# A hybrid encoder block on one core: first loads, value projection, attention values and last output chunk rearranged

## The chip, the cores and the metric

The kernel runs on one core of a Trainium2 chip. The metric is the device time of one execution in microseconds (us). Before the change the median of three runs is 1520.54 us (1519.51 to 1520.96).

## What is computed

The reference takes 512 tokens of width 1024. Everything is float32.

```
xn   = rms_norm(x, ln1)
proj = xn @ w_in                      # 1024 -> 2560: u 512, gate v 512, q 512, k 512, value 512
a    = gelu(u) * (w_s . rms_norm(gelu(v)) + b_s)        # block of 128 positions, 8 groups, masked
b    = softmax(q k^T / 8 + bias[rel]) value             # 8 heads of 64, chunk-causal, chunks of 64
x    = x + concat(a, b) @ w_out
x    = x + peer(rms_norm(x, ln2))     # 8 heads, top 16 of 128x128 experts, rows of two 16384x1024 tables
```

The change touches everything up to `w_out`; the expert part (`peer`) is left as it was.

## The kernel before, in words

The tokens are four tiles of 128 (t = 0 to 3); the model width is eight slices of 128 (k = 0 to 7). A product at full precision is written as three float32r matmuls on high and low parts (`mm3`, lines 117 to 121): a weight block of 128 x 1024 is loaded by SP's queue into `raw` (3 buffers), ScalarE makes `hi` (line 103), VectorE makes `lo` = `raw` - `hi` (line 104); `hi` and `lo` have 5 buffers each. A buffer is written again only when the matmuls that read it are done, so line 103 can wait for TensorE.

1. **Start.** SP's queue loads the gain row `g1`, the first tile of x, three weight blocks and the second tile of x, in this order (lines 185 to 192). `norm_transposed` (lines 131 to 151) squares a tile on ScalarE (137), makes 1/rms on VectorE and ScalarE (126 to 128), scales it on VectorE (`xs`, 140), transposes it on TensorE (145) and splits it into `xh` and `xl` (149, 150).
2. **Projections.** q goes token tile by token tile (lines 199 to 204). k and the values go through `token_major` (169): the loop over k is outside, four PSUM tiles are open at once, and the results are copied out at the end. Between k and the values stands the head norm of q and k (207 to 224): square, sum per head, 1/rms, scale (`qn`), eight transposes, copies to `qkT`.
3. **Gate values.** `gate_values` projects the gate input with `token_major` (96 `mm3` matmuls), then gelu and norm.
4. **Attention and gated product, interleaved** (lines 361 to 380). A step is one token tile and two heads; there are 16. TensorE's order is the program's (`manual_schedule`): in iteration i it does the scores of step i, a piece of the gated projection (iterations 0 to 7) or of the spatial product (8 to 11), the transposes of the weights of step i-2, and the values of step i-3. The softmax weights `pe` are not normalised; `values` multiplies them with `v_sb`, 64 columns wide, and after eight heads VectorE divides by the row sums into `o` (300). `mixed` transposes `o` (312) and splits it into `mh`, `ml`. Four gelus of 512 columns (353) stand behind the spatial product in the program.
5. **Output product.** Two chunks of 512 columns with `token_major`, each added to x on VectorE (402); then the second `norm_transposed` into `xbh`, `xbl`, on which routing (the first step of the expert part) waits.

Outside `manual_schedule` a scheduler sets each engine's order when the program is built, by priorities and its own cost estimates. An engine takes its instructions strictly in that order. What is written where in the program therefore moves instructions of all engines, also those of untouched lines.

Of the kernel before, what the change touches and what calls it, by code (L numbers as in the profile page):

```python
# [8 lines left out]
F32 = mybir.dt.float32  # L9
# [5 lines left out]
ALU = mybir.AluOpType  # L15
# [55 lines left out]
def hybrid_block(tc, x, ln1, w_in, gng, wsT, bsb, qkg, bias, w_out, ln2, wq, skT, uT, ud, vd, out):  # L71
    nc = tc.nc
    ctx = ExitStack()
    with ctx:
# [94 lines left out]
        def token_major(lh, ll, w, evac):  # L169

            pss = [pa() if t < 3 else pu() for t in range(TT)]
            for k in range(KT):
                for t in range(TT):
                    tok = slice(t * P, (t + 1) * P)
                    mm3(pss[t], (lh[:, k, tok], ll[:, k, tok]), w(k), k == 0, k == KT - 1)
            for t in range(TT):
                evac(t, pss[t])


        with tc.tile_pool(name="prea", bufs=1) as prea:  # L180
# [4 lines left out]
            nc.sync.dma_start(g1, bcast_rows(ln1, D))  # L185
            x_t = []
            for t in range(TT):
                xt = prea.tile([P, D], F32, name="x_t", tag="xq", bufs=4)
                nc.sync.dma_start(xt, x_r[t])
# [9 lines left out]
            for t in range(TT):  # L199
                ps = pu()  # L200
                tok = slice(t * P, (t + 1) * P)
                for k in range(KT):
                    mm3(ps, (xh[:, k, tok], xl[:, k, tok]), w0(k), k == 0, k == KT - 1)
                nc.scalar.copy(qk[t][:, 0:CW], ps)
            token_major(xh, xl, chunk_of(w_in, 2 * WA // CW + 1, CW),
                        lambda t, ps: nc.scalar.copy(qk[t][:, CW:2 * CW], ps))
            for t in range(TT):
# [8 lines left out]
                                        r[:, :, None].to_broadcast([P, 16, 64]), op=ALU.mult)  # L216
                for half in range(2):
                    ps = pa()
                    for j in range(4):
                        nc.tensor.transpose(ps[:, j * P:(j + 1) * P],  # L220
                                            qn[:, (4 * half + j) * P:(4 * half + j + 1) * P], ident)
                    nc.scalar.activation(qkT[:, 4 * half:4 * half + 4, t * P:(t + 1) * P],
                                         ps.rearrange("p (j t) -> p j t", t=P), AF.Copy,
                                         scale=qkgt[:, half:half + 1])
            token_major(xh, xl, chunk_of(w_in, 4 * WA // CW, CW),
                        lambda t, ps: nc.scalar.copy(v_sb[t], ps))


        with tc.tile_pool(name="preb", bufs=1) as preb:
# [34 lines left out]
            def weights(t, h, ps):  # L264
# [9 lines left out]
                                     accum_out=st[:, 1, h:h + 1])  # L274
                pes[t, h] = pe
# [11 lines left out]
            def values(t, h):  # L287
                if h == 0:
                    pvs[t] = pa()
                pv = pvs[t]  # L290
                pT = pTs.pop((t, h))
                hd = slice(h * 64, (h + 1) * 64)
# [3 lines left out]
                if h == HB - 1:  # L296
                    r = preb.tile([P, HB], F32, name="rs", tag="rs", bufs=2)
                    nc.vector.reciprocal(r, sts[t][:, 1, :])
                    o = preb.tile([P, WA], F32, name="o", tag="o", bufs=2)
                    nc.vector.tensor_tensor(o.rearrange("p (h d) -> p h d", d=64),  # L300
                                            pv.rearrange("p (h d) -> p h d", d=64),
                                            r[:, :, None].to_broadcast([P, HB, 64]), op=ALU.mult)
                    os[t] = o

            os = {}

            def mixed(t):

                o = os.pop(t)
                ps = pa()  # L310
# [3 lines left out]
                pv = ps.rearrange("p (k t) -> p k t", t=P)  # L314
                nc.scalar.copy(mh[to], pv)
                nc.vector.tensor_tensor(ml[to], pv, mh[to].bitcast(F32), op=ALU.subtract)
# [26 lines left out]
            def spatial():  # L343
# [8 lines left out]
                for m in range(4):  # L352
                    nc.scalar.activation(ugT[:, m, :], ugT[:, m, :], AF.Gelu_apprx_tanh)
# [10 lines left out]
            with tc.manual_schedule(engines={mybir.EngineType.PE}):  # L364
                for i in range(len(steps) + LAG + 3):
# [7 lines left out]
                    if 0 <= i - LAG - 1 < len(steps):  # L373
                        t, hs = steps[i - LAG - 1]
                        for h in hs:
                            values(t, h)
# [14 lines left out]
        with tc.tile_pool(name="prec", bufs=1) as preb:  # L391
# [7 lines left out]
            for c in range(D // CW):  # L399
                cs = slice(c * CW, (c + 1) * CW)  # L400
                token_major(mh, ml, chunk_of(w_out, c, CW),
                            lambda t, ps: nc.vector.tensor_tensor(x2[t][:, cs], x2[t][:, cs], ps, op=ALU.add))
# [353 lines left out]
```

## Time and profile before

| | before |
|---|---|
| median of 3 runs | 1520.54 us |
| the profiled execution | 1516.51 us |
| its span (first to last instruction) | 1514.7 us |
| TensorE busy | 1469.0 us, 97% |
| VectorE busy | 1118.7 us, 74% |
| ScalarE busy | 624.3 us, 41% |
| GpSimd busy | 474.8 us, 31% |

A busy share counts the time in which an instruction of the engine was under way. Matmuls overlap, so TensorE's throughput is read from the distance between the starts of successive matmuls, not from the length of one. A bracket at the end of a timeline row gives the idle time of that engine just before the row, and what ended it.

### The profile page before, as it was taken

How to read it: one execution, taken by the hardware profiler on the slowest of the kernel's cores; microseconds unless marked ns; L12 is line 12 of the kernel's file. 1: busy time of each engine (PE TensorE's matmuls, PEld its weight loads, DVE VectorE, ACT ScalarE, POOL GpSimd, SP SyncE). 2: the span in 40 equal slices, each digit the busy share in tenths (PEclk: the TensorE clock that was granted, in tenths of full speed). 3: DMA queues.
4: the chain of work that ended last, by engine and by line, in shares of the span. 5: the costliest groups of instructions: out<-in, count | busy, mean ns of one | idle time of the engine just before them, and what ended most of it. 6: DMA issues, size and time to landing. Idle time of an engine off the chain costs nothing.

```text
span 1514.7 us, 21441 instructions
## 1 busy us (share of the span) xinstructions
PE 1469.0 (97%) x7817; PEld 1315.6 (87%) x7817; DVE 1118.7 (74%) x2095; ACT 624.3 (41%) x1163; POOL 474.8 (31%) x322
## 2 busy tenths in 40 slices
PE   7899998999989999999999999999999999999998
PEld 5787887888879989999999999999999999998887
DVE  5425626999999986788777777777776877766773
ACT  5439715434446655333333333333333333333331
POOL 0000000000016753054444544444553444443420
PEclk9999999999999999999999999999999999999999
DMA  5341144223336879899898889888888888877881
GB/s 180 112 167 45 53 142 143 92 82 115 101 108 181 231 233 295 320 355 357 315 328 292 316 312 334 301 323 326 292 317 320 319 315 320 311 243 248 312 283 68
DMA packets 151721, 360.02 MB, mean 238 GB/s; under 512 B 11008, under 2 KB 71424, under 8 KB 151616
## 3 DMA queue, kind: packets, MB, share of 16 engines
q1 hardware_dynamic: 114528, 223.64, 43.5%
q0 software_dynamic: 37088, 135.02, 24.4%
q8 instruction: 61, 1.00, 0.3%
q14 instruction: 44, 0.36, 0.1%
HBM read 328.73 MB, written 29.88 MB: 237 GB/s over the span
## 4 chain that ended last, share of the span: by engine, by line
PE 62%; DMA 1%; DVE 0%; ACT 0%; issue 0%; POOL 0%; DVEq 0%; SPq 0%; ACTq 0%
PE pa L683 12%; PE pa L684 12%; PE pa L687 11%; PE pu L119 9%; PE pu L121 9%; PE pu L120 9%; PE pa L577 2%; DMA gd<-gst 1%; DMA gc<-gd 0%; ACT gst L582 0%; POOL bm L571 0%; DVE lo L104 0%; DVE bm L570 0%; ACT hi L103 0%; DVE wl L673 0%
## 5 line engine op out<-in xcount | busy, mean ns | idle before, releaser
L103 ACT ACTIVATE hi<-raw 128x1024 fp32r<-128x1024 f32 x300 | 317.1, 1058 | 538.0 <-PE pu L120 245.1
L104 DVE TENSOR_TENSOR lo<-raw,hi 128x1024 fp32r<-128x1024 f32 x300 | 369.6, 1233 | 173.1 <-ACT hi L103 168.3
L119 PE MATMUL pu<-xbh,hi 128*128 128x384 f32 x1024 | 346.6, 339 | 5.3 <-ACT act L432 5.3
L121 PE MATMUL pu<-xbh,lo 128*128 128x384 f32 x1024 | 345.4, 337 | 0.0
L120 PE MATMUL pu<-xbl,hi 128*128 128x384 f32 x1024 | 345.2, 337 | 0.0
L683 PE MATMUL pa<-hi,wh 128*128 128x512 f32 x768 | 299.2, 390 | 1.1 <-ACT wh L672 1.1
L684 PE MATMUL pa<-lo,wh 128*128 128x512 f32 x768 | 299.0, 389 | 0.0
L626 POOL DMA_INDIRECT row<-in_ud,eint x128 | 188.4, 1472 | 267.0 <-DVE row L628 237.1
L637 POOL DMA_INDIRECT row<-in_vd,eint x128 | 191.5, 1496 | 233.2 <-DVE acc L639 204.0
L687 PE MATMUL pa<-hi,wl 128*128 128x512 f32 x768 | 236.6, 389 | 0.5 <-DVE wl L673 0.5
L119 PEld LDWEIGHTS pu<-xbh,hi 128*128 128x128 f32 x1024 | 192.8, 188 | 8.2 <-ACT act L432 6.2
L120 PEld LDWEIGHTS pu<-xbl,hi 128*128 128x128 f32 x1024 | 192.6, 188 | 1.8
L121 PEld LDWEIGHTS pu<-xbh,lo 128*128 128x128 f32 x1024 | 192.6, 188 | 0.0
L571 POOL TENSOR_TENSOR bm<-bm,gt 128x1024 f32<-128x1024 f32 x48 | 91.1, 1897 | 301.1 <-DVE bm L570 301.1
L639 DVE SCALAR_TENSOR_TENSOR acc<-row,hw,acc 128x1024 f32<-128x1024 f32 x128 | 163.8, 1280 | 13.1 <-DMA row<-in_vd,eint 13.0
L687 PEld LDWEIGHTS pa<-hi,wl 128*128 128x128 f32 x768 | 144.1, 188 | 30.9 <-DVE wl L673 0.8
L683 PEld LDWEIGHTS pa<-hi,wh 128*128 128x128 f32 x768 | 144.2, 188 | 29.6 <-ACT wh L672 1.4
L684 PEld LDWEIGHTS pa<-lo,wh 128*128 128x128 f32 x768 | 144.2, 188 | 28.4
L628 DVE SCALAR_TENSOR_TENSOR row<-row,xb 128x1024 f32<-128x1024 f32 x128 | 155.8, 1219 | 11.7 <-DMA row<-in_ud,eint 11.6
L673 DVE TENSOR_TENSOR wl<-act,wh 128x768 fp32r<-128x768 f32 x64 | 61.2, 958 | 114.4 <-ACT wh L672 114.4
L672 ACT ACTIVATE wh<-act 128x768 fp32r<-128x768 f32 x64 | 54.0, 846 | 152.7 <-PE pa L684 150.8
L577 PE MATMUL pa<-bm,am 128*128 128x128 f32 x768 | 94.3, 276 | 5.4 <-POOL bm L571 3.6
(174 smaller groups left out, 1649.8 us busy)
## 6 DMA issues: line engine op xcount, KB each, us to landing
raw<-in_uT SPq DMA_DIRECT2D x128, 512.0 KB, 5.1
raw<-in_vd SPq DMA_DIRECT2D x128, 512.0 KB, 4.9
gd<-gst SPq DMA_DIRECT2D x48, 512.0 KB, 5.3
gc<-gd SPq DMA_DIRECT2D x32, 768.0 KB, 8.4
raw<-in_w_in SPq DMA_DIRECT2D x20, 512.0 KB, 4.2
raw<-in_wq SPq DMA_DIRECT2D x16, 512.0 KB, 4.5
raw<-in_w_out SPq DMA_DIRECT2D x8, 512.0 KB, 3.6
x_t<-in_x SPq DMA_DIRECT2D x4, 512.0 KB, 5.4
```

The costliest lines, as they stand in the source:

```text
L103: nc.scalar.activation(hi, raw, AF.Copy)
L104: nc.vector.tensor_tensor(lo, raw, hi.bitcast(F32), op=ALU.subtract)
L119: nc.tensor.matmul(ps, lh[0], rh[0], start=first, stop=False)
L120: nc.tensor.matmul(ps, lh[0], rh[1], start=False, stop=False)
L121: nc.tensor.matmul(ps, lh[1], rh[0], start=False, stop=last)
L626: nc.gpsimd.indirect_dma_start(out=row, out_offset=None, in_=ud, in_offset=bass.IndirectOffsetOnAxis(ap=eint[:, j:j + 1], axis=0))
L628: nc.vector.scalar_tensor_tensor(row, row, 1.0, xb0, op0=ALU.mult, op1=ALU.mult, accum_out=hw[:, j:j + 1])
L637: nc.gpsimd.indirect_dma_start(out=row, out_offset=None, in_=vd, in_offset=bass.IndirectOffsetOnAxis(ap=eint[:, j:j + 1], axis=0))
L639: nc.vector.scalar_tensor_tensor(acc0, row, hw[:, j:j + 1], acc0, op0=ALU.mult, op1=ALU.add)
L683: nc.tensor.matmul(accs[t][half], wh[:, b, tok], w[b][0][:, ds_], start=first, stop=False)
L684: nc.tensor.matmul(accs[t][half], wh[:, b, tok], w[b][1][:, ds_], start=False, stop=False)
L687: nc.tensor.matmul(accs[t][half], wl[:, b, tok], w[b][0][:, ds_], start=False, stop=last)
```

## The change

Five edits. The first tile of x is loaded as two halves, by SP's and by ScalarE's queue, and `g1` goes to GpSimd's queue. The value projection is done token tile by token tile inside the loop of the head norm, ahead of each tile's transposes. Each head's weights are divided by their sum right after the exponential (a reciprocal on VectorE, a scaling on GpSimd); the values of two heads are then computed transposed, the head's 64 value columns as the stationary operand, into the two halves of the partitions, so that `o` and its transposes go. The four gelus become one of 2048 columns. The second output chunk is done token tile by token tile.

```diff
-            nc.sync.dma_start(g1, bcast_rows(ln1, D))
...
+                if t == 0:
+
+                    nc.sync.dma_start(xt[:, 0:512], x_r[t][:, 0:512])
+                    nc.scalar.dma_start(xt[:, 512:D], x_r[t][:, 512:D])
+                    nc.gpsimd.dma_start(g1, bcast_rows(ln1, D))
+                else:
+                    nc.sync.dma_start(xt, x_r[t])
...
+            wv = chunk_of(w_in, 4 * WA // CW, CW)
             for t in range(TT):
...
+                ps = pu()
+                tok = slice(t * P, (t + 1) * P)
+                for k in range(KT):
+                    mm3(ps, (xh[:, k, tok], xl[:, k, tok]), wv(k), k == 0, k == KT - 1)
+                nc.scalar.copy(v_sb[t], ps)
                 for half in range(2):
...
-            token_major(xh, xl, chunk_of(w_in, 4 * WA // CW, CW),
-                        lambda t, ps: nc.scalar.copy(v_sb[t], ps))
...
+                nc.vector.reciprocal(st[:, 1, h:h + 1], st[:, 1, h:h + 1])
+                nc.gpsimd.tensor_scalar(pe[:, :nk], pe[:, :nk], st[:, 1, h:h + 1], None, op0=ALU.mult)
...
-                    nc.tensor.matmul(pv[:, hd], pT[:, j * P:(j + 1) * P], v_sb[j][:, hd],
-                                     start=j == 0, stop=j == t)
...
+                    for h, pT in zip(hs, pTh):
+                        nc.tensor.matmul(pv[rows_of(h), pair], v_sb[j][:, h * 64:(h + 1) * 64],
+                                         pT[:, j * P:(j + 1) * P], start=j == 0, stop=j == t)
...
-                for k in range(4):
-                    nc.tensor.transpose(ps[:, k * P:(k + 1) * P], o[:, k * P:(k + 1) * P], ident)
...
-                for m in range(4):
-                    nc.scalar.activation(ugT[:, m, :], ugT[:, m, :], AF.Gelu_apprx_tanh)
+                nc.scalar.activation(ugT, ugT, AF.Gelu_apprx_tanh)
...
+            token_major(mh, ml, chunk_of(w_out, 0, CW), residual(0))
+            token_major(mh, ml, chunk_of(w_out, 1, CW), residual(1), True)
```

With its last argument `token_major` runs the loop over t outside, one PSUM tile at a time. How the change moves instructions is shown at three places.

VectorE at the start, before (`rstd` is 1/rms of a tile, `xs` the scaled tile):

```order
L126 TENSOR_SCALAR rstd_142<-ss_139 128x1
L128 RECIPROCAL rstd_142<-rstd_142 128x1
L140 SCALAR_TENSOR_TENSOR xs_146<-x_t_104,rstd_142,g1_102 128x1024
L104 TENSOR_TENSOR lo_108<-raw_106,hi_107 128x1024
L104 TENSOR_TENSOR lo_114<-raw_112,hi_113 128x1024
```

VectorE at the start, in the changed kernel (`rstd_166` and `xs_170` are of the second tile):

```order
L126 TENSOR_SCALAR rstd_143<-ss_140 128x1
L128 RECIPROCAL rstd_143<-rstd_143 128x1
L104 TENSOR_TENSOR lo_109<-raw_107,hi_108 128x1024
L104 TENSOR_TENSOR lo_115<-raw_113,hi_114 128x1024
L104 TENSOR_TENSOR lo_121<-raw_119,hi_120 128x1024
L126 TENSOR_SCALAR rstd_166<-ss_163 128x1
L128 RECIPROCAL rstd_166<-rstd_166 128x1
L140 SCALAR_TENSOR_TENSOR xs_147<-x_t_103,rstd_143,g1_102 128x1024
L104 TENSOR_TENSOR lo_127<-raw_125,hi_126 128x1024
L140 SCALAR_TENSOR_TENSOR xs_170<-x_t_131,rstd_166,g1_102 128x1024
```

The scaling of the first tile has moved from third place to behind three weight splits and the 1/rms of the second tile. On TensorE the second tile's transposes have moved ahead too: from behind 24 matmuls of the first tile to behind one.

ScalarE in the changed kernel at the end of the gated projection, iterations 7 to 9 (`pe` a head's exponential, `pT` its transposed copy, `hi_1810` a block of `w_out`):

```order
L285 ACTIVATE pe_1201,st_1049<-sc_1197,st_1049 128x256
L103 ACTIVATE hi_1810<-raw_1809 128x1024
L285 ACTIVATE pe_1209,st_1049<-sc_1205,st_1049 128x256
L298 COPY pT_1229<-pu_1226 128x256
L298 COPY pT_1234<-pu_1231 128x256
L354 ACT_TABLE_LOAD
L354 ACTIVATE ugT_95<-ugT_95 128x2048
L285 ACT_TABLE_LOAD
L285 ACTIVATE pe_1252,st_1243<-sc_1248,st_1243 128x384
L285 ACTIVATE pe_1260,st_1243<-sc_1256,st_1243 128x384
L298 COPY pT_1277<-pu_1274 128x256
```

Before, the same place had a gelu of 512 columns and no `hi` in front of it; the other three gelus stood earlier, each between two table loads.

VectorE at the end of the second output chunk, in the changed kernel (last two tiles of the second norm):

```order
L401 TENSOR_TENSOR x2_1677<-x2_1677,pu_1885 128x512
L126 TENSOR_SCALAR rstd_1990<-ss_1987 128x1
L104 TENSOR_TENSOR lo_2064<-raw_2062,hi_2063 128x1024
L128 RECIPROCAL rstd_1990<-rstd_1990 128x1
L104 TENSOR_TENSOR lo_2136<-raw_2134,hi_2135 128x1024
L140 SCALAR_TENSOR_TENSOR xs_1994<-x2_1677,rstd_1990,g2row_1671 128x1024
L401 TENSOR_TENSOR x2_1679<-x2_1679,pu_1911 128x512
L441 MEMSET bits_2049 128x1 x6
L104 TENSOR_TENSOR lo_2199<-raw_2197,hi_2198 128x1024
```

Four splits of the next weights (the fourth is a few rows on, before the last tile's reciprocal) now stand between the last two tiles' norm steps; before, there was one. From the routing on, all engines have the order they had.

## Rows read from the trace of the kernel before

**Rows 1.** Page, part 1: busy time, share of the span and instructions of each engine.

```profile
PE 1469.0 (97%) x7817; PEld 1315.6 (87%) x7817; DVE 1118.7 (74%) x2095; ACT 624.3 (41%) x1163; POOL 474.8 (31%) x322
```

**Rows 2.** Busy time by stretch of 20 us: stretch, length, engines, PEclk, DMA share, GB/s.

```profile
60.00:80.00 20.00, 14.03 (x68) 11.23 (x68) 12.36 (x17) 11.56 (x21) 0.53 (x1) 0.83 0.12 37
...
220.00:240.00 20.00, 12.56 (x58) 10.28 (x57) 12.91 (x29) 10.07 (x19) 0.00 (x0) 0.91 0.64 224
```

**Rows 3.** Instructions by tile: x_t issued at 3.2 us, its time to landing.

```profile
DMA to landing us min/median/max: 8.8/8.8/8.8
```

**Rows 4.** Timeline of the start: start us, us, engine line operation.

```profile
3.20 0.57 SPq L189 DMA_DIRECT2D x_t<-in_x  x1
6.64 1.06 ACT L137 ACTIVATE junk<-x_t 128x1024 bf16<-128x1024 f32 x1 [4.38 <-DMA x_t<-in_x]
...
8.44 1.28 DVE L140 SCALAR_TENSOR_TENSOR xs<-x_t,rstd,g 128x1024 f32<-128x1024 f32 x1
...
9.87 1.94 PE L145 MATMUL pa<-ident,xs 128*128 128x128 f32 x8 [9.87 <-DVE xs L140]
...
13.24 0.63 PE L119 MATMUL pu<-hi,xh 128*128 128x512 f32 x1
...
14.52 0.63 PE L119 MATMUL pu<-hi,xh 128*128 128x512 f32 x1
...
15.74 1.22 DVE L104 TENSOR_TENSOR lo<-raw,hi 128x1024 fp32r<-128x1024 f32 x1 [1.28 <-ACT hi L103]
...
20.25 0.50 PE L119 MATMUL pu<-hi,xh 128*128 128x512 f32 x1 [0.24 <-ACT xh L149]
```

**Rows 5.** Timeline of TensorE, head norm to first scores.

```profile
65.35 1.06 PE L220 MATMUL pa<-ident,qn 128*128 128x128 f32 x8
...
76.89 1.94 PE L220 MATMUL pa<-ident,qn 128*128 128x128 f32 x8 [2.59 <-DVE qn L214]
...
116.18 0.49 PE L258 MATMUL pa<-qkT 64*128 64x128 f32 x4
```

**Rows 6.** Timeline of TensorE in the attention.

```profile
147.61 0.60 PE L282 MATMUL pu<-ident,pe 128*128 128x128 f32 x4
...
150.26 1.09 PE L347 MATMUL pa<-wst_t,vn 128*64 128x128 f32 x16
151.29 0.66 PE L282 MATMUL pu<-ident,pe 128*128 128x128 f32 x4
...
154.58 0.66 PE L282 MATMUL pu<-ident,pe 128*128 128x128 f32 x4
...
175.59 1.90 PE L294 MATMUL pa<-v_sb,pT 128*128 128x64 f32 x16
177.33 0.61 PE L312 MATMUL pa<-ident,o 128*128 128x128 f32 x4
```

**Rows 7.** Timeline of ScalarE and GpSimd; and two lines by source (min/median/max ns).

```profile
149.18 1.28 ACT L353 ACT_TABLE_LOAD   x1
...
154.10 0.62 ACT L284 COPY pT<-pu 128x256 f32<-128x256 f32 x2
...
L509 ACT COPY tree<-cand x8: 1932/1940/1949, 270.2 to 429.3; 128x2048 f32<-128x2048 f32 x8
...
L571 POOL TENSOR_TENSOR bm<-bm,gt x48: 1894/1897/1900, 449.6 to 578.0; 128x1024 f32<-128x1024 f32 x48
...
82.55 0.52 POOL L232 MEMSET wst_t<- 64x512 f32 x1 [2.34 <-DMA wst_t<-in_wsT]
```

**Rows 8.** Timeline of TensorE, second output chunk to routing.

```profile
218.16 0.39 PE L119 MATMUL pa<-hi,mh 128*128 128x512 f32 x1
...
228.82 0.39 PE L121 MATMUL pu<-hi,ml 128*128 128x512 f32 x1
233.29 3.25 PE L145 MATMUL pa<-ident,xs 128*128 128x128 f32 x16 [4.09 <-issue]
...
244.32 0.40 PE L120 MATMUL pa<-xbl,hi 128*128 128x512 f32 x1
```

More of the change, by code (lines that the diff above doesn't have):

```diff
@@ L167, in hybrid_block, with token_major @@
         ugT = pre.tile([P, 4, S], F32, name="ugT")
-        def token_major(lh, ll, w, evac):
+        def token_major(lh, ll, w, evac, by_tile=False):
+            if by_tile:
+                for t in range(TT):
+                    ps = pu()
+                    tok = slice(t * P, (t + 1) * P)
+                    for k in range(KT):
+                        mm3(ps, (lh[:, k, tok], ll[:, k, tok]), w(k), k == 0, k == KT - 1)
+                    evac(t, ps)
+                return
             pss = [pa() if t < 3 else pu() for t in range(TT)]
@@ L198, in hybrid_block @@
             qk = [prea.tile([P, D], F32, name="qk", tag="xq", bufs=4) for t in range(TT)]
[L199 to L204, printed above, removed]
+            token_major(xh, xl, w0, lambda t, ps: nc.scalar.copy(qk[t][:, 0:CW], ps), True)
             token_major(xh, xl, chunk_of(w_in, 2 * WA // CW + 1, CW),
                         lambda t, ps: nc.scalar.copy(qk[t][:, CW:2 * CW], ps))
+            wv = chunk_of(w_in, 4 * WA // CW, CW)
             for t in range(TT):
@@ L216, in hybrid_block @@
                                         r[:, :, None].to_broadcast([P, 16, 64]), op=ALU.mult)
+                ps = pu()
+                tok = slice(t * P, (t + 1) * P)
+                for k in range(KT):
+                    mm3(ps, (xh[:, k, tok], xl[:, k, tok]), wv(k), k == 0, k == KT - 1)
+                nc.scalar.copy(v_sb[t], ps)
                 for half in range(2):
@@ L374, in hybrid_block @@
                         t, hs = steps[i - LAG - 1]
-                        for h in hs:
-                            values(t, h)
+                        values(t, hs)
                     if 0 <= i - LAG - 2 < len(steps) and steps[i - LAG - 2][1][1] == HB - 1:
@@ L398, in hybrid_block, with residual @@
                 x2.append(xt)
-            for c in range(D // CW):
+            def residual(c):
                 cs = slice(c * CW, (c + 1) * CW)
-                token_major(mh, ml, chunk_of(w_out, c, CW),
-                            lambda t, ps: nc.vector.tensor_tensor(x2[t][:, cs], x2[t][:, cs], ps, op=ALU.add))
+                return lambda t, ps: nc.vector.tensor_tensor(x2[t][:, cs], x2[t][:, cs], ps, op=ALU.add)
+            token_major(mh, ml, chunk_of(w_out, 0, CW), residual(0))
+            token_major(mh, ml, chunk_of(w_out, 1, CW), residual(1), True)
             for t in range(TT):
```

22 lines of the change are left out of this document (5 added, 17 removed).

## The prediction, made before the changed kernel was run

> **What bounds the kernel now.** I first read the busy shares: TensorE is at 97% [rows 1], so time can only come from fewer matmul slots or from its few gaps. The stretches of 20 us then say where the gaps are: in the part that is touched (0 to 245 us) TensorE is short of work at the very start, in 60 to 80 us (6 us missing, granted clock 0.83) and in 220 to 240 us (7.4 us missing) [rows 2]. The timeline of each gap says who is waited for: at the start the first scaled tile on VectorE [rows 4], then the head norm's `qn` [rows 5], at the end the second norm [rows 8]. Between the gaps TensorE is the bound, one 512-column matmul every (228.82 - 218.16) / 47 = 0.2268 us [rows 8]; where it has just stood still it takes (14.52 - 13.24) / 3 = 0.43 us [rows 4], the lower of its two clock levels, 1.2 instead of 2.4 GHz. After 245 us no engine's order changes, so what reaches routing earlier ends earlier.
>
> **The start, a loss.** The first tile is first in two queues, no longer behind `g1`, and may land over 1 us earlier. That gains nothing, because VectorE now scales it only behind the 1/rms of the second tile. That tile is issued at 3.20 and lands 8.8 us later, at 12.0 [rows 3, 4]. Five transfers of its own size stood ahead of it; the same five, `g1` among them, stand ahead of it or beside it now, so I take 12.0 again (and 10.5 as the least: one transfer less at their pace of 8.8 / 6 = 1.5 us, if `g1` comes behind it). From a tile's square to its scaling takes 8.44 - 6.64 = 1.8 us, and to the transposes another 9.87 - 8.44 = 1.43 us [rows 4]. So `xs` of tile 0 starts at 13.8 instead of 8.44, its transposes at 15.2 instead of 9.87. VectorE then does one more split (1.22 us [rows 4]) and `xs` of tile 1, 15.1 to 17.6. TensorE has one matmul and then tile 1's transposes in its order: 17.6 to 19.5 at the low clock (1.94 us for eight [rows 4]). 23 matmuls are left until the point that stood at 20.25 before: two or three at 0.43 us and the rest at 0.2268 make 5.6 us, 25.1. Loss 4.8 us. Bounds: 3.5 (second tile at 10.5) to 6.5 (all matmuls of the first 5 us at the low clock). Nothing behind it hides this: from there to the head norm TensorE has no gap to give.
>
> **Value projection among the head norms, the main gain.** From tile 0's transposes (65.35) to the first scores (116.18) stand 171 matmuls and four groups of eight transposes, 50.8 us [rows 5]. 171 x 0.2268 = 38.8, and 4 x 1.1 us for the transposes with the switch (1.06 in its row [rows 5]) = 4.4: 7.6 us are idle or at the low clock. With 24 matmuls (5.4 us) ahead of each tile's transposes, longer than the (76.89 - 65.35) / 3 = 3.8 us in which a `qn` came [rows 5], TensorE no longer waits, and the clock has no reason to fall. Gain 7.6 us, bounds 6.5 and 8.5. The weight blocks of the values are split during the k projection, since buffers come free with its loop over k.
>
> **Attention values.** The old form costs (177.33 - 175.59) / 16 = 0.109 us per instruction [rows 6]; one matmul is two instructions, so there are 160. The nearest row to the new form is the spatial product, also 64 stationary columns into alternating halves: (151.29 - 150.26) / 16 = 0.064 us, the switches into and out of it included [rows 6]. 160 x 0.045 = 7.2 us. The 16 transposes of `o` go too: four groups at some 0.5 us (0.61 with its tail [rows 6]), 2.0 us. The Trainium skill (TensorEngine Tiling (Array Packing), Theoretical Speedup) gives up to 2x for a dimension of 64 or less. By the page the values would cost half, a saving of 8.7 us instead of 7.2, an estimate from that page's factor; its Key Properties also say that a change of tiling mode drains the engine, which the 0.064 us holds already.
>
> Against this stand two new waits. (a) A head's weights now pass reciprocal and GpSimd before their transposes. GpSimd's multiply of 1024 elements takes 1897 ns [rows 7], so 512 cost at most 0.95 us scaled down and no less than the 0.52 us of a memset of that size; I take 0.9. At the second head of step 0 TensorE already waited for the exponential, so there the chain shows: 0.7 us. Later a step's weights are ready two iterations (5 us) ahead. (b) ScalarE. Call G the end of the gated product, before 147.61 [rows 6]. In the new order a `hi` that needs the weight buffer of the last gated matmul stands ahead of the exponential, the copies of step 5 and the long gelu. It starts at about G + 0.25 and delays them by 1.06 us. From a gelu's table load to the next copied transpose took 154.10 - 149.18 = 4.92 us with a gelu of 0.6 and a cast of 0.6 in it [rows 7]; with 2048 columns (1.94 us [rows 7]) and no cast it is 5.7. So the copy of step 6 is done at about G + 0.25 + 1.06 + 0.6 + 0.55 + 5.7 + 0.3 = G + 8.5. TensorE needs its PSUM buffer for the transposes of step 7 at G + 5.7 (before: 154.58 - 147.61 = 7.0 [rows 6], less two batches of values and one `mixed`). It waits 2.8 us. The three other gelus and their table loads take no ScalarE time any more, but TensorE did not wait for them. Sum: 7.2 + 2.0 - 0.7 - 2.8 - 0.3 (small waits for copies when steps shorten) = 5.4 us. Bounds: 2.5 and 8.5.
>
> **Second output chunk.** Before, from the last matmul (228.82 + 0.23) to a running routing took until 244.32: 15.3 us [rows 8]. Now tiles 0 and 1 are transposed inside the chunk (2 us of TensorE plus a short wait, 2.5 us). But tile 2's `xs` stands behind two splits that wait for weight buffers of the last token tile, and tile 3's chain (add, square, two more splits, reciprocal, scale, transposes at the low clock, cast, split) starts only behind tile 2's. Adding these durations I get about 12.4 us from the last matmul, so 15.3 - 2.5 - 12.4 = 0.4 us gained; bounds -2 and 4.
>
> **Sum.** -4.8 + 7.6 + 5.4 + 0.4 = 8.6 us, against the profiled execution of 1516.5: 1507.9. The median of the runs is 4.0 us above that execution, and I subtract the same from it: 1520.5 - 8.6 = 1512 us.
>
> **Rivals.**
> - *The start gains as meant* (second tile very early, or the splits cost nothing): +1.5 instead of -4.8, time 1505.5. Against it: the order of VectorE is fixed and the 12.0 us are a row. Chance 0.10.
> - *GpSimd and VectorE get in each other's way.* Each scaling would hold off a VectorE instruction with two SBUF inputs (eight of 0.7 us in iterations 8 to 12, plus splits), and the softmax chain queues behind those. At 0.95 us each, half of them on the path: 4 us, time 1516. The Trainium skill (SBUF — State Buffer, Terms) says that the two engines share a port pair as an exclusive lock held for a whole instruction. No row here shows two such instructions in conflict. Chance 0.18, with a slower GpSimd multiply (1.5 us for 512) in it.
> - *Slower: GpSimd becomes the bound.* The scalings of the last eight steps are 14 times that of 512 columns. They must fit into the 25 us of these steps and may add the 8.6 us gained: from (25 + 8.6) / 14 = 2.4 us for 512 columns on, the kernel is slower. At 3 us it is 14 x 3 - 25 = 17 us against 8.6, time 1529. Against it: 2.5 times the multiply's row. Chance 0.05.
> - *It doesn't come through*: the gaps are filled, but the waits at G, the start and the last norm each cost their upper bound: time 1519 to 1520. Chance 0.07.
>
> **How the numbers follow.** The forecast keeps 0.60, with 1508 to 1516 as its own range (start 3.5 to 6.5, gelu wait 1 to 4). Reaching to the start that gains and to the port conflict gives 1505 to 1518. A measurement of this kernel tells some 0.2% (3 us) from no change. Faster by more: forecast, the first rival and two thirds of the second, 0.80. Within: the rest of the second, the last and a little of the forecast, 0.14. Slower: 0.06.
>
> **What would show it.** Right: first transposes near 15 us and the 25th `mm3` matmul near 25 us; no idle time of TensorE ahead of the transposes of `qn`; values at 0.064 us per instruction; one wait of about 3 us for a copy of `pT` behind the gelu; the gap behind the output product shorter by 2 to 3 us, but its matmuls later by as much. Wrong: first transposes before 11 us; a scaling over 1.5 us on GpSimd, or transposes waiting for GpSimd in many steps; no wait behind the gelu; routing starting over 12 us earlier than before, or not earlier at all.

## The result, and the profile of the changed kernel

The changed kernel takes 1511.07 us (median of six runs, 1508.17 to 1513.77); the kernel before, on the same chip, 1518.54 us (six runs, 1516.5 to 1520.96). The ratio is 0.9949, 95% interval 0.9934 to 0.9965: faster by 7.5 us. The forecast was 1512, 8.6 us less. The time is right; of the four terms one is far off and two are too small, which the total hides.

The profiled execution of the changed kernel is the longest of its six (1513.77 us, span 1512.0), that of before the shortest of its six (1516.51). So the two profiles differ by 2.7 us only, and the ends of the traces can't be compared. What can be compared is the start of the same TensorE instruction. I count the `mm3` matmuls in the timeline of TensorE; the 769th is the first one of the second head of routing, behind everything that the change touches. From it to the end of the execution it takes 1516.51 - 264.63 = 1251.9 us before and 1513.77 - 259.22 = 1254.6 us after, and between 1250.6 and 1255.5 us in the profiles of all twelve kernels of this study, with no order by their edits. The marks ahead of it repeat better, so each term is read between marks:

| stretch | before | changed | gain | predicted |
|---|---|---|---|---|
| start, to the 193rd matmul (q and k are done) | 60.28 | 65.37 | -5.1 | -4.8 |
| to the first scores (384 matmuls done) | 55.90 | 47.24 | +8.7 | +7.6 |
| attention, to the 529th matmul | 80.22 | 79.92 | +0.3 | +5.4 |
| to the 769th matmul | 68.23 | 66.69 | +1.5 | +0.4 |
| sum | 264.63 | 259.22 | +5.4 | +8.6 |

The marks give 5.4 us; the medians' 7.5 us lie within the spread of the rest.

Most stretches repeat well, two places do not. Over the kernels of this study that share the code of a stretch, the value projection takes 47.24 to 47.32 us (eleven kernels), the attention 79.88 to 79.94 (four), and the way from the 529th matmul to the first one of routing, the 673rd, 44.39 to 44.40 (seven, two of them with the slices of the first chunk in another order). The start does not repeat like that. The 193rd matmul stands at 63.98 to 65.59 us in the five kernels with the changed start, and at 59.55 to 60.32 in the seven others. Nor do routing's first eight matmuls, behind the wait for the last norm. They take 2.70 to 3.44 us in the same seven kernels, with the granted clock lower the longer they take. Here they are in the changed kernel and in run 3 (the clock is the third number from the end):

```profile
236.93:239.95 3.02, 3.02 (x10) 2.36 (x10) 1.36 (x2) 0.58 (x1) 0.00 (x0) 0.61 0.07 30
```

```profile
234.90:238.34 3.44, 3.44 (x9) 2.68 (x9) 1.36 (x2) 0.59 (x1) 0.00 (x0) 0.53 0.04 17
```

So differences in the first row of the table, and in the last one (66.37 to 67.27 us in those seven kernels), are known to about 1 us only.

The page of the changed kernel, part 1 (against [rows 1]), then its busy time by stretch of 20 us, with the granted clock in the first column behind the brackets (against [rows 2]; the last line is the kernel before):

```profile
PE 1463.5 (97%) x7801; PEld 1305.9 (86%) x7801; DVE 1119.7 (74%) x2119; ACT 616.7 (41%) x1154; POOL 515.9 (34%) x355
```

```profile
60.00:80.00 20.00, 20.00 (x98) 16.72 (x97) 12.82 (x18) 11.99 (x20) 0.00 (x0) 1.00 0.20 56
140.00:160.00 20.00, 17.87 (x143) 11.62 (x143) 14.36 (x45) 16.70 (x37) 9.35 (x9) 0.91 0.17 54
220.00:240.00 20.00, 13.36 (x59) 10.65 (x58) 12.77 (x24) 9.36 (x16) 0.00 (x0) 0.83 0.50 172
```

```profile
140.00:160.00 20.00, 20.00 (x158) 15.48 (x154) 15.72 (x45) 19.59 (x46) 0.00 (x0) 1.00 0.24 81
```

The shares hardly move. In 60 to 80 us TensorE (first pair) is now full and its clock stays up; instead 140 to 160 us have a hole, with the clock at 0.91, where TensorE was busy throughout before, at 1.00.

The start, timeline of all engines (against [rows 4]):

```profile
4.66 1.06 ACT L137 ACTIVATE junk<-x_t 128x1024 bf16<-128x1024 f32 x1 [1.99 <-DMA x_t<-in_x]
...
6.26 0.16 DVE L128 RECIPROCAL rstd<-rstd 128x1 f32<-128x1 f32 x1 [0.27 <-ACT rstd L127]
7.20 1.23 DVE L104 TENSOR_TENSOR lo<-raw,hi 128x1024 fp32r<-128x1024 f32 x1 [0.78 <-ACT hi L103]
...
12.43 1.06 ACT L137 ACTIVATE junk<-x_t 128x1024 bf16<-128x1024 f32 x1 [0.24 <-DMA x_t<-in_x]
...
14.22 1.28 DVE L140 SCALAR_TENSOR_TENSOR xs<-x_t,rstd,g 128x1024 f32<-128x1024 f32 x1
...
15.65 1.94 PE L145 MATMUL pa<-ident,xs 128*128 128x128 f32 x8 [15.65 <-DVE xs L140]
```

The first tile is squared 2.0 us earlier (4.66 instead of 6.64) and its 1/rms stands at 6.42, but the scaling comes only behind the splits and the second tile (squared at 12.43). The forecast had 13.8 and 15.2 for scaling and transposes, which start at 14.22 and 15.65.

TensorE from the end of k to the first scores (against [rows 5]); from 60 us to the first scores no row has an idle time any more:

```profile
70.81 1.03 PE L234 MATMUL pa<-ident,qn 128*128 128x128 f32 x8
71.61 0.48 PE L119 MATMUL pu<-hi,xh 128*128 128x512 f32 x1
...
112.61 0.49 PE L270 MATMUL pa<-qkT 64*128 64x128 f32 x4
```

TensorE in the attention (against [rows 6]), and ScalarE and GpSimd beside it (against [rows 7]); the last fence groups GpSimd's scalings by shape (count, then busy us and mean ns of one, then idle time before them and its releasers):

```profile
124.31 0.33 PE L296 MATMUL pu<-ident,pe 128*128 128x128 f32 x1 [1.41 <-POOL pe L288]
...
140.38 0.60 PE L296 MATMUL pu<-ident,pe 128*128 128x128 f32 x4
140.91 0.44 PE L310 MATMUL pa<-pT,v_sb 128*64 128x128 f32 x4
141.28 0.70 PE L270 MATMUL pa<-qkT 64*128 64x256 f32 x4
...
148.93 0.92 PE L270 MATMUL pa<-qkT 64*128 64x384 f32 x4
149.78 1.09 PE L349 MATMUL pa<-wst_t,vn 128*64 128x128 f32 x16
153.01 0.72 PE L296 MATMUL pu<-ident,pe 128*128 128x128 f32 x4 [2.13 <-issue]
...
154.50 1.65 PE L270 MATMUL pa<-qkT 64*128 64x384 f32 x4
156.08 1.69 PE L349 MATMUL pa<-wst_t,vn 128*64 128x128 f32 x16
...
174.05 1.09 PE L310 MATMUL pa<-pT,v_sb 128*64 128x128 f32 x16
175.07 0.66 PE L296 MATMUL pu<-ident,pe 128*128 128x128 f32 x4
```

```profile
146.83 1.28 ACT L354 ACT_TABLE_LOAD   x1
148.13 1.91 ACT L354 ACTIVATE ugT<-ugT 128x2048 f32<-128x2048 f32 x1
150.05 1.28 ACT L285 ACT_TABLE_LOAD   x1
...
152.56 0.62 ACT L298 COPY pT<-pu 128x256 f32<-128x256 f32 x2
```

```profile
L288 POOL TENSOR_SCALAR pe<-pe,st 128x512 f32<-128x512 f32 x8 | 12.4, 1563 | 0.5 <-PE pu L296 0.2 <-PE pa L270 0.2
L288 POOL TENSOR_SCALAR pe<-pe,st 128x384 f32<-128x384 f32 x8 | 11.6, 1452 | 6.5 <-DVE st L287 5.6 <-DVE st L283 0.8
```

The values take (175.07 - 174.05) / 16 = 0.064 us per instruction, as forecast. The transposes at 153.01 follow the copies that start at 152.56, behind table load, gelu and table load. The profile names no releaser here; for the same wait in run 3 (2.09 us) it names ScalarE's copy of `pT`. And then the same scores that took 0.92 us at 148.93 take 1.65, the same spatial product 1.69 instead of 1.09: after the stop the granted clock falls, and from 153 to 157 us it is 0.62 on average, most of it at the lower of its two levels (fence below). GpSimd needs 1.56 us for 512 columns, not 0.9.

```profile
153.00:157.00 4.00, 3.99 (x26) 2.31 (x28) 2.86 (x11) 2.96 (x9) 3.34 (x4) 0.62 0.00 0
```

The second output chunk (against [rows 8]), its last two tiles, and below them the second wait of the kernel before:

```profile
228.61 1.09 PE L145 MATMUL pa<-ident,xs 128*128 128x128 f32 x8 [1.18 <-DVE xs L140]
...
235.16 1.94 PE L145 MATMUL pa<-ident,xs 128*128 128x128 f32 x8 [5.46 <-DVE xs L140]
```

```profile
239.90 3.23 PE L145 MATMUL pa<-ident,xs 128*128 128x128 f32 x16 [3.35 <-DVE xs L140]
```

Two waits, 1.18 and 5.46 us, where before there were 4.09 and 3.35. Routing starts (673rd matmul) at 236.93 instead of 242.95 us: from the 529th matmul to there it is 44.40 us instead of 46.55. Two matmuls of the first products that stood third and fourth in routing before stand later now, so TensorE's order is not quite the old one there; by the 769th the same ones are done.

### The profile page after: what moved, and what is told of

It reads as the page before. It is cut to its first block, busy times and chain, and to the rows that moved or that the text cites. A ratio compares the mean times of both kernels' runs of the same rounds, so it can differ in the third digit from the quotient of the medians.

```text
span 1512.0 us, 21509 instructions
## 1 busy us (share of the span) xinstructions
PE 1463.5 (97%) x7801; PEld 1305.9 (86%) x7801; DVE 1119.7 (74%) x2119; ACT 616.7 (41%) x1154; POOL 515.9 (34%) x355
## 4 chain that ended last, share of the span: by engine, by line
PE 63%; DMA 0%; ACT 0%; issue 0%; DVE 0%; POOL 0%; ACTq 0%; DVEq 0%
PE pa L685 12%; PE pa L686 12%; PE pa L689 12%; PE pu L121 9%; PE pu L120 9%; PE pu L119 9%; PE pa L579 2%; DMA gd<-gst 0%; ACT gst L584 0%; POOL bm L573 0%; DVE bm L572 0%; ACTq L674 0%; DVE wl L675 0%; ACT wh L674 0%; DVE res L712 0%
## 5 line engine op out<-in xcount | busy, mean ns | idle before, releaser
L628 POOL DMA_INDIRECT row<-in_ud,eint x128 | 195.0, 1524 | 275.6 <-DVE row L630 238.8
L639 POOL DMA_INDIRECT row<-in_vd,eint x128 | 188.4, 1472 | 222.3 <-DVE acc L641 202.4
L573 POOL TENSOR_TENSOR bm<-bm,gt 128x1024 f32<-128x1024 f32 x48 | 91.1, 1897 | 300.6 <-DVE bm L572 300.6
```

The lines of the kernel that those rows point to most:

```text
L628: nc.gpsimd.indirect_dma_start(out=row, out_offset=None, in_=ud, in_offset=bass.IndirectOffsetOnAxis(ap=eint[:, j:j + 1], axis=0))
L639: nc.gpsimd.indirect_dma_start(out=row, out_offset=None, in_=vd, in_offset=bass.IndirectOffsetOnAxis(ap=eint[:, j:j + 1], axis=0))
```

## The experiments

Ten kernels. "Changed kernel" is the one above; a time stands beside runs of the kernel before on the same chip.

**1. The start put back.** Lines 193 to 202 as they were:

```diff
+            nc.sync.dma_start(g1, bcast_rows(ln1, D))
...
-                if t == 0:
...
-                    nc.gpsimd.dma_start(g1, bcast_rows(ln1, D))
-                else:
-                    nc.sync.dma_start(xt, x_r[t])
+                nc.sync.dma_start(xt, x_r[t])
```

> The changed kernel with only the start put back: g1, then the whole first tile, on SP's queue. Marks are the starts of TensorE's n-th mm3 matmul, counted from the program's start. Theory: the changed start costs 5.1 us and nothing behind it hides any of that. Then the 193rd matmul starts at 60.3 us (65.37 in the changed kernel, 60.28 before), every later mark is earlier by the same 5.1 us (769th: 254.1 instead of 259.22), and the time falls by 5 us to some 1506 us. Rival: a later wait (a weight transfer, a store) takes some of it back; then the 769th mark is earlier by under 3 us.

Measured: 193rd matmul at 59.90, 769th at 253.47 (5.75 us earlier), 1508.2 us against 1518.04 (0.9926, 0.9905 to 0.9946). The stretches behind the start are as in the changed kernel (79.88 us of attention against 79.92; 66.45 us of the last stretch against 66.69). The start costs some 5 us, and nothing gives it back. Over all profiles the 193rd matmul stands at 64.9 us on average with the changed start and at 60.0 with the other; single pairs give 3.7 to 6.0.

**2. Two queues, but the gain row on SP's queue.**

```diff
-                    nc.gpsimd.dma_start(g1, bcast_rows(ln1, D))
+                    nc.sync.dma_start(g1, bcast_rows(ln1, D))
```

> The changed kernel with g1 on SP's queue, behind the first half of the first tile, instead of on GpSimd's; the tile still comes by two queues. In the program VectorE's scaling of the first tile then stands third again, ahead of the weight splits. Theory: the loss at the start is VectorE's order (the program's scheduler puts the scaling behind three splits because it takes g1 on GpSimd's queue to be late), and the two queues themselves cost nothing: first transposes between 8.0 and 9.9 us, 193rd matmul between 58.8 and 60.3 us, time 5 to 6.5 us under the changed kernel. Rival: the second queue slows the weight blocks, since the DMA engines are shared: first transposes early, but 193rd matmul at 61 us or later.

Timeline of this kernel's start:

```profile
6.85 1.29 DVE L140 SCALAR_TENSOR_TENSOR xs<-x_t,rstd,g 128x1024 f32<-128x1024 f32 x1 [0.66 <-DMA g<-in_ln]
...
8.28 1.94 PE L145 MATMUL pa<-ident,xs 128*128 128x128 f32 x8 [8.28 <-DVE xs L140]
...
11.06 0.79 PE L119 MATMUL pu<-hi,xh 128*128 128x512 f32 x1 [0.83 <-ACT xh L149]
...
19.88 0.50 PE L119 MATMUL pu<-hi,xh 128*128 128x512 f32 x1 [0.24 <-ACT xh L149]
```

With the scaling ahead of the splits again the first transposes come at 8.28 and the 193rd matmul at 59.91: the second queue for the tile is not the loss. This run puts back two things at once, VectorE's order and the queue of the gain row, and the row was late on GpSimd's queue. Its landing is on record in run 6, which has the changed start (scaling of the tiles; issue of the row; its time to landing):

```profile
L140 DVE SCALAR_TENSOR_TENSOR xs<-x_t,rstd,g x4: 1274/1277/1286, 13.9 to 23.2; 128x1024 f32<-128x1024 f32 x4
L200 POOL DMA_DIRECT2D g<-in_ln x1: 717/717/717, 1.5 to 1.5; - x1
DMA to landing us min/median/max: 8.5/8.5/8.5
```

The row is there at 10.0 us, and the scaling starts at 13.9, with all that it needs. So 3.9 of the 5.5 us of its delay are VectorE's order. The row's own landing would have held it to 10.0 instead of the 8.44 of the kernel before, 1.6 us; no run has that queue with the old order.

The second queue earns nothing either. The transposes are 1.3 us earlier than in run 1 (9.54), the first matmul 0.24 us (11.06 against 11.30), and the 25th matmul starts at 19.88 in both. Time 1507.06 us (0.9919, 0.9898 to 0.994).

**3. The division left out.** Lines 287 and 288 removed: the attention weights stay undivided, and nothing else divides them.

```diff
-                nc.vector.reciprocal(st[:, 1, h:h + 1], st[:, 1, h:h + 1])
-                nc.gpsimd.tensor_scalar(pe[:, :nk], pe[:, :nk], st[:, 1, h:h + 1], None, op0=ALU.mult)
```

> The changed kernel without the reciprocal and GpSimd's scaling: the division of the attention weights by their row sum is left out. Theory: of the attention's missing gain some 3 us are waits for GpSimd, which takes 1.54 us for 512 columns (0.9 in the prediction): the wait at the second head of step 0 falls from 1.41 to about 0.5 us, the waits of TensorE in front of the transposes behind 160 us go, and from the first scores (112.61) to the 529th matmul (192.53) it takes 2.5 to 3.5 us less than 79.9. The stop of 2.13 us at 150.9 us with the low clock behind it stays. Rival: the waits behind 160 us are ScalarE's copies of pT; then this stretch is shorter by under 1.5 us.

Measured: the wait at the second head of step 0 is 0.51 us instead of 1.41, but the stretch of the attention is 78.71 us, only 1.2 us less. The waits for `pT` behind 160 us stay (0.42 and 0.42 instead of 0.48 and 0.51). My theory fell, the rival holds: the reciprocal and the path over GpSimd cost 1.2 us together, 0.9 of it at step 0. That a scaling takes 1.56 us is hidden by the steps that lie between a weight and its transposes: from step 1 on TensorE waits for no scaling in the changed kernel. Time 1510.44 us (0.9936, 0.9915 to 0.9956).

**4. The gelu late.** Gelu, gate products and their splits are issued behind the last `mixed` copy on ScalarE; the first output chunk takes the attention's slices first.

```diff
-            for k in range(KT):
+            for k in ks:
...
+            with tc.issue_after(marks['mixed']):
+                gate_tail()
...
-            token_major(mh, ml, chunk_of(w_out, 0, CW), residual(0))
+            token_major(mh, ml, chunk_of(w_out, 0, CW), residual(0), ks=(4, 5, 6, 7, 0, 1, 2, 3))
```

> The changed kernel with the one long gelu, the gate products and their splits issued behind the last copy of the attention on ScalarE, and the first output chunk going through slices 4 to 7 (the attention's) before 0 to 3 (the gate's). Theory: the stop at 150.9 us is the table loads and the gelu in front of ScalarE's copies of pT, and the low clock behind it belongs to it: 2.13 + 1.6 us. Without it there is no stop and the granted clock stays 1.00 from 146 to 160 us, and the 529th matmul (192.53) comes 2 to 3.7 us earlier. Rival: GpSimd is the next bound, since its sixteen scalings of 384 and 512 columns take 24 of the 26.6 us from 152.4 to 179.0: then under 1.5 us come through, and TensorE's waits for pe grow instead.

Busy time of this kernel in the stretch that had the hole:

```profile
140.00:160.00 20.00, 20.00 (x186) 13.47 (x186) 15.27 (x54) 13.11 (x39) 12.65 (x11) 1.00 0.17 54
```

No hole, clock 1.00, and the attention takes 75.98 us, 3.94 us less. So the gelu's stop costs 3.9 us: 2.1 of idle time and the rest by the low clock behind it. GpSimd didn't become the bound. (The 769th matmul is 5.64 us earlier than in the changed kernel, but 1.4 us of that is the start, which this edit does not touch: 193rd at 63.98.) Time 1508.44 us (0.9928, 0.9907 to 0.9949).

**5. The value projection alone.** The kernel before with the loop of lines 226 to 230 as the only edit.

```diff
+            wv = chunk_of(w_in, 4 * WA // CW, CW)
             for t in range(TT):
...
+                for k in range(KT):
+                    mm3(ps, (xh[:, k, tok], xl[:, k, tok]), wv(k), k == 0, k == KT - 1)
+                nc.scalar.copy(v_sb[t], ps)
...
-            token_major(xh, xl, chunk_of(w_in, 4 * WA // CW, CW),
-                        lambda t, ps: nc.scalar.copy(v_sb[t], ps))
```

> The kernel before with one edit of the five: the value projection token tile by token tile inside the loop of the head norm. Theory: this edit alone is worth 8.7 us (from the 193rd matmul to the first scores 47.2 us instead of 55.9), and nothing behind it hides it: first scores at 107.5 us (116.18 before), all later marks 8.7 us earlier, 769th at 255.9 (264.63), time 1509 to 1510 us. Rival: the projection's weight blocks or PSUM buffers are not there in time without the other edits; then there are waits of TensorE between 60 and 85 us, and the first scores come after 109 us.

The first scores in TensorE's timeline of this kernel:

```profile
107.38 0.49 PE L262 MATMUL pa<-qkT 64*128 64x128 f32 x4
```

193rd matmul at 60.14, first scores at 107.38: 47.24 us, the changed kernel's own value to the hundredth. The 529th matmul is 8.8 us earlier than before, the 769th only 8.0 (256.67): the last stretch, which this edit does not touch, takes 69.06 instead of 68.23 us, part of the scatter told of above. 1510.62 us against 1519.18 (0.9949, 0.9931 to 0.9966). Within the intervals this one edit is worth as much as all five.

**6. The second output chunk put back.**

```diff
-            token_major(mh, ml, chunk_of(w_out, 1, CW), residual(1), True)
+            token_major(mh, ml, chunk_of(w_out, 1, CW), residual(1))
```

> The changed kernel with only the second output chunk put back to the loop over k outside. Theory: from the 529th matmul (192.53) to the 769th (259.22) the tile-by-tile form takes 66.7 us against 68.2 before; put back, it takes 68.2 again, so the 769th comes 1.5 us later, at 260.8, and the time rises by 1.5 us. Rival: the 1.5 us come from elsewhere (the first tiles' norms are hidden either way, what counts is the last tile's chain); then the 769th moves by under 0.5 us.

From the 529th to the 769th matmul it takes 260.50 - 192.29 = 68.21 us against 66.69, 1.5 us more. To the first matmul of routing it takes 46.99 us against 44.40: there the tile-by-tile form is worth 2.6 us, and the difference is mostly how soon the clock is back behind the wait. Routing's first eight matmuls, two narrower ones among them, take 1.84 us in this run at a granted clock of 1.00, against 3.02 us at 0.61. 1514.53 us (0.9972, 0.9961 to 0.9982).

**7. Start put back and gelu late.** The edits of runs 1 and 4 together.

> The changed kernel with the start put back and with the late gelu (gate products behind the attention, slices 4 to 7 first). Theory: the two gains add, since TensorE is the bound between them: first scores at 107.1, 529th matmul 9.4 to 9.6 us earlier than in the changed kernel (183.1 instead of 192.53), 769th at 249.6, time some 1502 to 1504 us. Rival: without the 3.9 us stop something else is late in the attention or at the first output chunk (a weight block, the gate's slices); then the 769th is at 251 us or later.

529th matmul at 183.52 (9.0 us earlier), 769th at 250.40 (8.8 us earlier; its start lies 0.4 us behind that of run 1, 60.32 against 59.90 at the 193rd). The gains add. 1504.37 us (0.9904, 0.9883 to 0.9924).

**8. And the last norm ahead of routing's splits.** On top of run 7:

```diff
-            nc.scalar.activation(hi, raw, AF.Copy)
-            nc.vector.tensor_tensor(lo, raw, hi.bitcast(F32), op=ALU.subtract)
+            with held("ACT"):
+                nc.scalar.activation(hi, raw, AF.Copy)
+            with held("DVE"):
+                nc.vector.tensor_tensor(lo, raw, hi.bitcast(F32), op=ALU.subtract)
```

`held` issues them behind the last tile's square root and scaling, for routing's first head only.

> The same as the run with the start put back and the late gelu, and the splits of routing's first weight blocks issued behind the last tile's square root (ScalarE) and behind its scaling (VectorE). Theory: the gap of 5.46 us in front of the last tile's transposes holds three splits of 1.2 us on VectorE and one or two of 1.06 us on ScalarE that nobody needs yet; without them the last scaling comes some 3 us earlier after the last matmul, and the 769th matmul 2 to 3 us earlier than in that run. Rival: routing's first matmuls need these blocks at once, so that the wait only moves behind the transposes: under 1 us, or a loss.

The last tile in the timeline of this kernel (`L149` scales, `L111` splits, `L154` transposes):

```profile
221.45 1.29 DVE L149 SCALAR_TENSOR_TENSOR xs<-x,rstd,g2row 128x1024 f32<-128x1024 f32 x1
222.65 2.36 DVE L111 TENSOR_TENSOR lo<-raw,hi 128x1024 fp32r<-128x1024 f32 x2
...
222.88 1.94 PE L154 MATMUL pa<-ident,xs 128*128 128x128 f32 x8 [4.04 <-DVE xs L149]
```

One wait of 4.04 us is left of 1.18 and 5.46. From the 625th matmul (205.28) to the first one of routing it is 19.37 us against 21.83 in run 7, 2.5 us less, as expected. To the 769th (247.91) it is 42.63 us against 44.32: 1.7 us. The other 0.8 us go in routing's first matmuls; two splits now stand between the last scaling and the last `xbl`, but that they are the reason is not shown, and the scatter there is as large. 1502.4 us (0.989, 0.9873 to 0.9908), the shortest time of the study, 8.7 us under the changed kernel by the medians and 0.6% by the two ratios.

**9. Values of two steps together.** On top of run 8, with five instead of three `pT` buffers:

```diff
-                    if 0 <= i - LAG - 1 < len(steps):
-                        t, hs = steps[i - LAG - 1]
-                        values(t, hs)
+                    if 0 <= i - LAG - 1 < len(steps) and (i - LAG - 1) % 2:
+                        for t, hs in steps[i - LAG - 2:i - LAG]:
+                            values(t, hs)
```

> The kernel of the run with the last norm first, with the values of two steps together in every second iteration (and two more pT buffers). Theory: in the changed kernel each group of transposes takes 0.09 to 0.1 us longer than before because the 64-column values follow it (four transposes 0.53 instead of 0.44 us, the next start less this one), a switch that the prediction left out; with half the switches the stretch from the first scores to the 529th matmul is 0.7 to 1 us shorter than 75.94. Rival: the longer groups are a wait for the weights pe or for PSUM, not the switch: then the stretch is within 0.3 us of 75.94, or longer since the copies of pT bunch up.

TensorE's timeline of this kernel in the attention (`L300` transposes, `L314` values, `L274` scores):

```profile
134.22 0.60 PE L300 MATMUL pu<-ident,pe 128*128 128x128 f32 x4
134.75 0.66 PE L314 MATMUL pa<-pT,v_sb 128*64 128x128 f32 x8
...
138.84 0.60 PE L300 MATMUL pu<-ident,pe 128*128 128x128 f32 x4
139.37 0.92 PE L274 MATMUL pa<-qkT 64*128 64x384 f32 x4
```

The stretch is 76.01 us against 75.94: nothing. The rows say why. Four transposes take 0.53 us ahead of values (134.22 to 134.75) and 0.53 us ahead of scores (138.84 to 139.37), so half the groups of values saves no transpose time; the values themselves fall from 11.35 to 10.12 us over the stretch, and the waits of TensorE rise from 2.27 to 4.08 us, for copies of `pT` and for a scaling. Every group of transposes still has another tile shape behind it, so the run doesn't test whether the shape is the cause; rows of the kernel before do (next section). 1502.6 us (0.9892, 0.9876 to 0.9909).

**10. Four gelus again.** Line 354 back to its loop of four in the changed kernel.

```diff
-                nc.scalar.activation(ugT, ugT, AF.Gelu_apprx_tanh)
+                for m in range(4):
+                    nc.scalar.activation(ugT[:, m, :], ugT[:, m, :], AF.Gelu_apprx_tanh)
```

> The changed kernel with the four gelus of 512 columns instead of the one of 2048. Theory: it is the long gelu that makes TensorE stop at 150.9 us: with four, only 0.6 instead of 1.9 us of gelu stand between the two table loads there, the stop is under 1 us, the low clock behind it does not come, and the stretch from the first scores to the 529th matmul is 2 to 3.5 us shorter than 79.9. Rival: the two table loads (1.28 us each) and the weight copies in front are what counts, so that a stop of 1 to 2 us with the low clock stays, and with three more pairs of table loads the stretch is shorter by under 1 us or longer.

The stop is 1.09 us and the clock stays at 1.00 (140 to 160 us), but an earlier gelu now makes a wait of 1.44 us at 129.78, and one at 167.14 is 1.02 instead of 0.48 us. The attention takes 79.40 us, 0.5 us less. So neither side holds whole: the low clock is gone, as the theory said, but other waits for ScalarE take its place, and the time is the rival's. (The profile names GpSimd's scaling for the wait at 129.78; the exponential ahead of it starts at 127.36, behind a gelu and a table load.) Whether one gelu or four stand inside the attention hardly matters; taking them out of it does (run 4). 1512.44 us (0.9961, 0.9947 to 0.9976).

## Why the prediction was right, and where it was wrong

**The start: right.** -4.8 was forecast, -5.1 came (about 5 over all profiles), for the reason given: at 14.22 the scaling follows at once on the 1/rms of the second tile, some 4 us behind the landing of the gain row as run 6 has it. That this row is late on its new queue was not in the forecast; it would count only with the old order. The forecast's sign, the 25th matmul near 25 us, came at 27.28, for a reason of order: two more groups of transposes (23.23 and 25.71) stand ahead of it, 1.9 us from start to start. The rival that the start gains as meant was priced at +1.5; with the right order no gain shows (59.91 against 59.90 at the 193rd matmul), and the 25th matmul starts at 19.88 in either case, though the tile's transposes come 1.3 us earlier.

**Value projection: the mechanism right, the size 1.1 us too small.** 8.7 us against 7.6, just over the upper bound of 8.5. The term "4 x 1.1 us for the transposes with the switch" took the length of the row as its cost. A group of eight costs 71.61 - 70.81 = 0.80 us from start to start; 4 x 0.3 us is the difference.

**Attention values: wrong.** +0.3 came instead of +5.4, outside its bounds of 2.5 to 8.5. TensorE's time from the first scores to the 529th matmul, by what it did (from each group's start to the next one's, idle time apart):

| us | before | changed | gelu late (run 4) |
|---|---|---|---|
| values | 17.97 | 11.57 | 11.36 |
| transposes of `o` | 1.89 | 0 | 0 |
| transposes of the weights | 9.66 | 11.66 | 11.57 |
| scores and spatial product | 15.93 | 17.34 | 15.94 |
| `mm3` matmuls | 34.25 | 34.82 | 34.85 |
| idle | 0.52 | 4.53 | 2.26 |
| sum | 80.22 | 79.92 | 75.98 |

The columns before and changed differ by 0.3 us in all. Step by step:
- "7.2 values": 6.4 came. The 0.064 us hold for a group of 16; a group of four takes (141.28 - 140.91) / 4 = 0.093 each.
- "2.0 for `o`": 1.9.
- "-0.7 wait at step 0": 0.9. The scaling of 512 columns was put at 0.9 us with 0.95 as upper bound; it takes 1.56. That row was mis-sized by 1.7 times, and still the whole path costs 1.2 us only (run 3). A scaling over 1.5 us was among the forecast's own signs of being wrong, and not a good one: the rival with GpSimd at 1.5 us had the duration right and the consequence wrong.
- "-2.8 wait behind the gelu": the wait is 2.1 us, but TensorE falls to its lower level behind it. Run 4 puts both at 3.9. I had used the low clock for the start and forgot it here.
- "-0.3 small waits": the two waits for `pT` are 1.0 us.
- Not in the sum at all: the transposes of the weights take 2.0 us more. Before, four of them took 143.59 - 143.15 = 0.44 us up to the values (fence below), now 140.91 - 140.38 = 0.53. The values had the tile shape of the transposes (128\*128), now they have another (128\*64). I wrote that the 0.064 us "hold already" the switches; they hold the one behind the values only. That the shape of what follows sets this, and no wait for a weight, is seen in the kernel before (second fence below): four transposes of `o`, behind no scaling of GpSimd, take 149.42 - 148.88 = 0.54 us ahead of scores (64\*128) and 177.77 - 177.33 = 0.44 [rows 6] ahead of other transposes. And with no division at all (run 3) four transposes take 0.53 us ahead of values. The Trainium skill (TensorEngine Tiling (Array Packing), Key Properties) says that changing the tiling mode drains TensorE; these 0.1 us per group agree with it. The rows show that the cost goes with the shape; that it is a drain they don't show. Some 16 groups at 0.09 us make 1.5 of the 2.0 us; the other 0.5 are not taken apart.
- The `mm3` matmuls take 0.6 us more: at the end of the attention three short groups of them now stand between weights and values (1, 3 and 2 matmuls in 0.47, 0.94 and 0.66 us, 0.2 to 0.3 more each than at 0.2268 us per matmul).

TensorE in the attention of the kernel before, at the place of 140.38 to 141.28 above, and the transposes of `o`:

```profile
143.15 0.60 PE L282 MATMUL pu<-ident,pe 128*128 128x128 f32 x4
143.59 0.56 PE L294 MATMUL pa<-v_sb,pT 128*128 128x64 f32 x4
```

```profile
148.88 0.61 PE L312 MATMUL pa<-ident,o 128*128 128x128 f32 x4
149.42 0.92 PE L258 MATMUL pa<-qkT 64*128 64x384 f32 x4
...
177.77 1.21 PE L282 MATMUL pu<-ident,pe 128*128 128x128 f32 x8
```

**Second output chunk: right sign, too small.** +1.5 against +0.4 at the 769th matmul, inside -2 to 4; up to routing's first matmul it is 2.2 us (2.6 by run 6), and the forecast counted to a row just behind that one. The chunk's own matmuls take 2.1 us more, against 2.5 in the forecast. The mis-sized term is the way from the last matmul to routing. The forecast had it 2.9 us shorter (15.3 to 12.4); from the start of the chunk's last matmul to that of routing's first it went from 14.13 to 9.88 us, 4.2 shorter. Which row of the forecast's chain was too long stays open. Run 8 shows that 2.5 us of what is left are splits of weights for routing, and that the norm need not wait for them.

**The total** came out by luck: the error of the attention (-5.1) was in part made up by value projection and chunk (+2.2), and the medians show 2 us more than the marks, within the spread of the rest. It lies in the forecast's own range, but one of the four reasons for it does not hold. The slower rival (GpSimd as the bound from 2.4 us per 512 columns on) stayed away at 1.56.

## What to carry to other kernels

Read a change between marks of the same instruction, not from the ends of two traces: here most stretches repeat to some 0.1 us, where the times of one kernel scatter by 3 to 5. The first one and the last one repeat to about 1 us only; profiles of several kernels that share the code of a stretch show which kind it is. When an engine is the bound, the cheapest gain is other ready work in front of its waits (one loop moved: 8.7 us); a rewrite that shortens its instructions must be costed with the switches next to them and with the clock behind every new stop. A long instruction of a side engine that switches tables belongs where nobody waits for that engine, and a transfer moved to another queue can change an order that a scheduler derives from it.

## What the runs showed of the hardware that was not expected

GpSimd's scaling by a per-partition factor takes 0.61 us for 128 columns, 0.92 for 256, 1.24 for 384 and 1.54 for 512 where nothing disturbs it (six in 9.26 us), 2.4 ns per further column, more than its product of two full operands (1897 ns for 1024 [rows 7], 1.9 ns per column).

GpSimd and VectorE instructions take longer beside each other. The splits of the gate products on VectorE, with the division left out, so without GpSimd (first row), and in the changed kernel (second):

```profile
L358 DVE TENSOR_TENSOR ml<-vn,mh x4: 682/685/687, 152.2 to 162.7; 128x512 fp32r<-128x512 f32 x4
```

```profile
L360 DVE TENSOR_TENSOR ml<-vn,mh x4: 682/768/1009, 154.0 to 164.4; 128x512 fp32r<-128x512 f32 x4
```

One of four takes 1009 instead of 685 ns, and GpSimd's scaling of 384 columns 1452 ns on average where it takes 1.24 us undisturbed. The Trainium skill (SBUF — State Buffer, Terms) describes a lock on a port pair that the two engines share, which would do this; the rows agree but don't show the lock itself. Run 3 bounds the price here: it is part of 1.2 us, of which 0.9 are the chain at step 0.
